# A hybrid attention and RWKV-7 layer: output weights split in two parts during the dense projections, kept in DRAM and loaded in parts in attention's first two tiles

## Chip, cores and metric

The kernel runs on one core of a Trainium2 chip. The metric is the device time of one execution in microseconds; a kernel's figure is the median of its timed runs. The engines named below are PE (TensorE, matmuls, with its weight loads PEld), DVE (VectorE), ACT (ScalarE), POOL (GpSimd) and SP (SyncE), which here only issues DMAs.

## What is computed

One layer on 1024 tokens of width 1024: RMSNorm, one input projection, eight heads of sparse attention beside eight heads of RWKV-7 time mixing, each times a SiLU gate, one output projection, a residual add and a last RMSNorm. Cut to what matters here:

```python
h = rms_norm(x, norm_g)
q, kc, vc, ks, vs, kw, vw, gl, g_nsa, rwkv_in, g_rwkv = split(h @ w_in)
o_nsa = nsa_mixer(q, kc, vc, ks, vs, kw, vw, gl, ...) * silu(g_nsa)
o_rwkv = rwkv7_mixer(rwkv_in, ...) * silu(g_rwkv)
mix = concatenate([o_nsa, o_rwkv])          # 1024 wide
return rms_norm(x + mix @ w_out, final_g)   # w_out: 1024 x 1024
```

All dense products are done in two parts: a float32 matrix is rounded to a high part (type fp32r), and the low part is the float32 matrix less the high one. A product takes three matmuls: high times high, low times high, high times low.

## The kernel before

**Projections.** After the norm, 29 groups of 128 output columns run on PE (`wda k0 k1 r0 r1 v0 v1 r2 k2 r3 k3 ...`), each 48 matmuls: two halves of 512 tokens, eight blocks of 128 input rows, three matmuls each. `Filler.weights` (L365) looks at the count of matmuls issued in the running group and serves the next one. At 2 it issues `fetch` of the first half of the next weights (a DMA of 256 KB into `wr`, which has one buffer), at 22 `split` and the fetch of the second half, at 40 the second `split`. `split` (L339) is an ACT copy (`k1h<-k1r`) and a DVE subtraction (`k1l<-k1r,k1h`), both made to wait for that matmul. The raw buffer is single, so a fetch waits for the subtraction ahead of it: four links, fetch, split, fetch, split, turn round once in each group. The second half of a group's weights is first used by its 13th matmul. Around these groups lie the RWKV pieces of the first head pairs (`wkv_elementwise`, `wkv_products`), and later, in the eight chains of the RWKV state, the groups fill PE between the links.

**Attention.** Eight tiles of 128 queries in the order 1, 5, 4, 3, 6, 2, 7, 0 (L1396), each with two branches (b = 0 and 1). A step of a branch is scores (`pst`), exponentials on ACT (`prob`), values (`po`) and sums of exponentials on POOL (`acc`). Beside these steps lie side pieces, put in at given shares of the branch: row maxima of the next branch (`ps`, `pd` on PE, `bm` and `nm` on DVE, turned by PE as `pnm`), the compressed branch (`pcs`, `pct`), the end of the branch before (`pz`, `rr`, `wide` on POOL, turned by PE as `prt`), the RWKV half of the mix (`mix_rwkv`: loads `yr` and `sg`, a POOL product, two ACT copies, a DVE subtraction `ml`) and, from the third tile, the output product (`output`, L1138).

**Output weights.** `load_w_out` (L1102) brings the eight blocks of `w_out` as raw 512 KB tiles (`wor`, two buffers shared with the residual `xt`), makes the high part on ACT (`woh`) and the low part on POOL (`wol`), four blocks in each branch of the second tile (`side.add(wout, 4)`, L1493). The output products of the first tile, in the third, are the first to read them.

**Order.** PE's order in attention is that of the program. The order of the other engines comes from a scheduler, which works from a model of the times; on the chip it is fixed. Every DMA is issued by SP, in order, so a DMA whose data are not ready holds up all behind it.

## Time and profile before

| what | value |
|---|---|
| timed runs | 1052.12, 1043.89, 1053.36 us; median 1052.12 us |
| profiled execution, its own time | 1040.26 us |
| its span | 1038.5 us, mean granted clock 0.951 |
| busy in the span | PE 930.2 us (90%), DVE 584.0, POOL 448.2, ACT 335.5 |
| moved by DMA | 115.66 MB, mean 111 GB/s |
| projections before the chains | about 50 to 185 us |
| attention | about 640 to 1015 us |

The engines run side by side and wait for each other by semaphores. PE is the fullest. A page of the profile shows how busy each engine was in 40 slices of the span, the DMA rate and the clock granted to TensorE (1.00 is its upper level of 2.4 GHz, 0.50 its lower of 1.2). The timelines show every instruction with its start, and in brackets how long its engine had been idle before it and what ended that. The chain of waits is followed back from the last instruction to whatever released each step.

### The profile page before, as it was taken

To read this page: it belongs to the slowest core of one execution; us is meant where nothing else is said; L and a number is where in the kernel's file an instruction comes from. 1 tells how busy PE (TensorE), PEld (TensorE's weight loads), DVE (VectorE), ACT (ScalarE), POOL (GpSimd) and SP (SyncE) were. 2 spreads that over 40 slices of the span, in tenths; PEclk is the share of its full clock that TensorE was granted. 3 is DMA by queue.
4 is the path that set the end of the run, shared out by engine and by line. 5 is a ranking of instruction groups with operands and counts; after the bars stand their busy time and mean duration, and the time that the engine had idled before them with its cause. 6 is when DMAs were issued, how large, how long until landed. Compare 5 with 4: busy or idle time off the path is not lost.

```text
span 1038.5 us, 17087 instructions
## 1 busy us (share of the span) xinstructions
PE 930.2 (90%) x6353; PEld 658.6 (63%) x6353; DVE 584.0 (56%) x1245; ACT 335.5 (32%) x650; POOL 448.2 (43%) x732
## 2 busy tenths in 40 slices
PE   5999999989998999899669978689999999889976
PEld 4888777766676766677458756354565656455555
DVE  7533545555575657374424335677659856685544
ACT  5533233224233443243121212433333333224321
POOL 3100153466483847444521120577463555246521
PEclk9999999999999999799889988879999999899989
DMA  7433453424426453536476293741132312231121
GB/s 259 125 102 102 125 157 108 130 76 116 135 76 172 134 154 119 131 106 170 116 218 192 65 203 95 212 122 31 41 63 79 77 46 69 53 80 33 39 84 41
DMA packets 154429, 115.66 MB, mean 111 GB/s; under 512 B 54369, under 2 KB 132266, under 8 KB 154346
## 3 DMA queue, kind: packets, MB, share of 16 engines
q1 hardware_dynamic: 154346, 114.57, 40.3%
q8 instruction: 50, 0.82, 0.3%
q14 instruction: 33, 0.27, 0.1%
HBM read 76.19 MB, written 35.19 MB: 107 GB/s over the span
## 4 chain that ended last, share of the span: by engine, by line
PE 60%; DVE 10%; DMA 9%; POOL 7%; SPq 6%; issue 5%; ACT 2%; POOLq 0%; DVEq 0%; ACTq 0%
PE pout L113 7%; SPq L85 6%; PE pst L113 6%; PE po L113 5%; PE p_r L113 4%; PE p_k L113 3%; PE p_gn L113 3%; PE p_gr L113 3%; PE p_q L113 3%; PE pc L113 2%; POOL lt L586 2%; POOL ltmp L584 2%; PE ps L113 2%; PE pd L113 2%; PE pcm L113 2%
## 5 line engine op out<-in xcount | busy, mean ns | idle before, releaser
L584 POOL TENSOR_TENSOR ltmp<-la,lt 128x60 f32<-128x60 f32 (+24 forms) x248 | 83.7, 337 | 65.3 <-DMA la<-dA 42.7
L1042 ACT ACTIVATE prob<-pst 128x512 f32<-128x512 f32 x132 | 74.6, 593 | 109.9 <-PE pst L113 106.3
L1055 POOL TENSOR_TENSOR acc<-acc,prob 128x1024 f32<-128x1024 f32 x36 | 86.7, 2409 | 45.1 <-ACT prob L1042 44.9
L586 POOL TENSOR_TENSOR lt<-lt,ltmp 128x60 f32<-128x60 f32 (+24 forms) x248 | 87.6, 353 | 18.8
L113 PE MATMUL pst<-q,k 128*128 128x512 f32 (+1 forms) x264 | 82.3, 430 | 0.0
L994 DVE TENSOR_REDUCE bm<-ps 128x6 f32<-128x384 f32 (+1 forms) x106 | 63.5, 613 | 26.6 <-PE ps L113 26.0
L113 PE MATMUL po<-prob,vt 128*64 128x512 f32 x264 | 75.1, 648 | 0.0
L1055 POOL TENSOR_TENSOR acc<-prob 128x1024 f32<-128x1024 f32 x14 | 33.7, 2410 | 82.6 <-ACT prob L1042 82.6
L113 PEld LDWEIGHTS pst<-q,k 128*128 128x128 f32 (+1 forms) x264 | 48.9, 196 | 14.9 <-issue 5.7
L113 PE MATMUL pout<-woh,mh 128*128 128x512 f32 x128 | 57.6, 450 | 0.2 <-DVE xt L1153 0.2
L113 PE MATMUL ps<-k,q 128*128 128x384 f32 (+3 forms) x136 | 45.4, 386 | 7.7 <-DVE bm L994 3.7
L113 PE MATMUL pout<-wol,mh 128*128 128x512 f32 x128 | 51.3, 401 | 0.0
L113 PE MATMUL pout<-woh,ml 128*128 128x512 f32 x128 | 51.2, 400 | 0.0
L113 PEld LDWEIGHTS ps<-k,q 128*128 128x128 f32 x136 | 25.6, 205 | 35.2 <-DVE bm L994 14.3
L982 DVE TENSOR_REDUCE bm<-pd 128x8 f32<-128x512 f32 x40 | 27.4, 688 | 26.2 <-PE pd L113 26.0
L113 PEld LDWEIGHTS pout<-woh,mh 128*128 128x128 f32 x128 | 25.1, 196 | 20.7 <-issue 17.8
L683 ACT ACTIVATE x<-pc 64x128 f32<-64x128 f32 x32 | 8.7, 272 | 75.4 <-DVE x L682 75.2
L113 PE MATMUL pd<-k,q 128*128 128x128 f32 x160 | 31.1, 321 | 2.1 <-POOL k L868 2.1
L1077 POOL TENSOR_TENSOR wide<-rr,ones 128x512 f32<-128x512 f32 x16 | 17.1, 1068 | 36.1 <-DVE rr L1073 34.1
L1069 DVE TENSOR_REDUCE zz<-pz 128x4 f32<-128x512 f32 x32 | 21.8, 684 | 13.4 <-PE pz L1067 13.0
L1153 DVE TENSOR_TENSOR xt<-pout,xt 128x512 f32<-128x512 f32 x16 | 11.1, 691 | 32.4 <-PE pout L113 32.4
L113 PEld LDWEIGHTS pd<-k,q 128*128 128x128 f32 x160 | 25.9, 204 | 4.0 <-POOL k L868 2.4
(518 smaller groups left out, 2447.7 us busy)
## 6 DMA issues: line engine op xcount, KB each, us to landing
dM<-mix SPq DMA_DIRECT2D x24, 256.0 KB
q<-dQH SPq DMA_DIRECT2D x22, 256.0 KB
la<-dA SPq DMA_DIRECT2D x32, 128.0 KB
xt<-in_x_dram SPq DMA_DIRECT2D x8, 512.0 KB
out_dram<-xt SPq DMA_DIRECT2D x16, 256.0 KB
x<-in_x_dram SPq DMA_DIRECT2D x7, 512.0 KB
mixk<-dM SPq DMA_DIRECT2D x8, 256.0 KB
mixr<-dM SPq DMA_DIRECT2D x8, 256.0 KB
```

What stands on the lines that cost most here:

```text
L85: return nc.sync.dma_start(plain(o), plain(i))
L113: return T.matmul(o, l, r, start=start, stop=stop)
L584: G.tensor_tensor(tv, la[:, j:j + 1, j + 1:].to_broadcast([128, m, n]), lt[:, :m, j:j + 1].to_broadcast([128, m, n]), op=OP.mult)
L586: G.tensor_tensor(lt[:, :m, j + 1:], lt[:, :m, j + 1:], tv, op=OP.add)
L683: gate["A"] = A.activation(x1[1][HP[1], c:8:4, :], pv[HP[1], :, 64:128], AF.Copy)
L982: V.tensor_reduce(bm[:, g * 4:g * 4 + 4, j:j + 2], p.rearrange("p (r b c) -> p r b c", b=2, c=64), axis=AX.X, op=OP.max)
L994: V.tensor_reduce(bm[:, h0:h0 + n, j:j + 2 * w], p[:, :n * w * 128].rearrange("p (h b c) -> p h b c", h=n, c=64), axis=AX.X, op=OP.max)
L1042: A.activation(pr[:, g * 512:(g + 1) * 512], p, AF.Exp)
L1055: G.tensor_tensor(s, self.acc, pr, op=OP.add)
L1069: V.tensor_reduce(zz[:, g, :], p.rearrange("p (r k) -> p r k", r=4), axis=AX.X, op=OP.add)
L1077: G.tensor_tensor(wide, rr.rearrange("p r g -> p (r g)").unsqueeze(2).to_broadcast([128, 8, 64]), ones64.unsqueeze(1).to_broadcast([128, 8 ...
L1153: V.tensor_tensor(xt[:, hs], p, xt[:, hs], op=OP.add)
```

## The change

A new generator, `split_w_out`, reads `w_out` in 16 parts of 128 x 512, makes the high part on ACT and the low part on DVE, and stores both to DRAM (`dWH`, `dWL`). Its tiles take one turn of the three buffers of `g0`, `g1` and `ar`, which the RWKV pieces use later; the two column halves of a tile alternate, and the load of the next part is issued ahead of the split of this one. `Filler.weights` calls it at the counts 12 and 34 of every group after the first. In attention `load_w_out` now only loads the two parts of each block (512 KB each), two blocks in each branch of the first two tiles, each load made to wait for the last exponential issued (`last_exp`). The raw tile `wor`, the ACT copies and the POOL subtractions there are gone.

```diff
--- before.py
+++ after.py
@@ -225,6 +225,7 @@
     dY = dram.tile([4, 128, S], FT, name="dY")
     dM = [dram.tile([4, 128, S], FT, name=f"dM{i}") for i in range(3)]
     dSR = dram.tile([4, 128, S], FT, name="dSR")
+    dWH, dWL = (dram.tile([8, 128, D], FR, name=n) for n in ("dWH", "dWL"))
 
 
     hh = [pj.tile([128, 8, 512], FR, name=f"hh{i}") for i in range(2)]
@@ -361,8 +362,11 @@
 
         def __init__(self, groups):
             self.groups, self.at, self.gen, self.i, self.cut = groups, -1, None, 0, None
+            self.extra = iter(())
 
         def weights(self, ins):
+            if self.at > 0 and self.i in (12, 34):
+                next(self.extra, None)
             if self.at + 1 == len(self.groups):
                 return
             g = self.groups[self.at + 1]
@@ -789,6 +793,36 @@
                     dma(v[:, hf * 8:hf * 8 + 8, :], t[hf * 64:hf * 64 + n])
             yield
 
+
+    def split_w_out():
+
+
+        wn = w_out.rearrange("l (n x) c -> (l n) x c", x=512)
+        raw, wh, wl = (r2(t, 3, (128, 8, 2, 64)).rearrange("p a b c -> p (a b c)")
+                       for t in ("g0", "g1", "ar"))
+
+        def load(k, cs):
+            o = raw[:, cs]
+            if k < 4:
+                for g in range(2):
+                    r0 = g * 256 + k * 64
+                    dma(o[g * 64:g * 64 + 64], wn[0, r0:r0 + 64, cs])
+            else:
+                dma(o, wn[1, (k - 4) * 128:(k - 3) * 128, cs])
+
+        parts = [(k, slice(h, h + 512)) for k in (4, 5, 6, 7, 0, 1, 2, 3) for h in (0, 512)]
+        load(*parts[0])
+        yield
+        for n, (k, cs) in enumerate(parts):
+            if n < 15:
+                load(*parts[n + 1])
+            h_ = wh.bitcast(FR)[:, cs]
+            A.activation(h_, raw[:, cs], AF.Copy)
+            l_ = wl.bitcast(FR)[:, cs]
+            V.tensor_tensor(l_, raw[:, cs], wh[:, cs], op=OP.subtract)
+            dma(dWH[k][:, cs], h_)
+            dma(dWL[k][:, cs], l_)
+            yield
 
     def compress(b, w1, w2):
         kc = []
@@ -1039,7 +1073,7 @@
                 mm(p, K2[b, g][:, w], L["q2", b][:, gh, :], start=False, stop=mask is None)
                 if mask is not None:
                     mm(p, identb, maskb[:, mask:mask + 1, :].to_broadcast([128, 4, 128]), start=False)
-                A.activation(pr[:, g * 512:(g + 1) * 512], p, AF.Exp)
+                last_exp[0] = A.activation(pr[:, g * 512:(g + 1) * 512], p, AF.Exp)
 
         def values(self, kt):
             if kt == 0:
@@ -1099,20 +1133,13 @@
 
     wo_h, wo_l = {}, {}
 
+    last_exp = [None]
+
     def load_w_out():
-        wn = w_out.rearrange("l (n x) c -> (l n) x c", x=512)
         for k in (4, 5, 6, 7, 0, 1, 2, 3):
-            raw = f4([128, D], FT, "wor")
-            if k < 4:
-                for g in range(2):
-                    r0 = g * 256 + k * 64
-                    dma(raw[g * 64:g * 64 + 64, :], wn[0, r0:r0 + 64, :])
-            else:
-                dma(raw, wn[1, (k - 4) * 128:(k - 3) * 128, :])
-            h_, l_ = w4([128, D], FR, "woh"), w4([128, D], FR, "wol")
-            A.activation(h_, raw, AF.Copy)
-            G.tensor_tensor(l_, raw, h_.bitcast(FT), op=OP.subtract)
-            wo_h[k], wo_l[k] = h_, l_
+            wo_h[k], wo_l[k] = w4([128, D], FR, "woh"), w4([128, D], FR, "wol")
+            for t, d in ((wo_h[k], dWH), (wo_l[k], dWL)):
+                behind(dma(t, d[k]), last_exp[0])
             yield
 
     xr = x.rearrange("b (n p) d -> (b n) p d", p=128)
@@ -1278,6 +1305,7 @@
         cp = pool(cmp_stack, "cp", "right")
 
     cp = None
+    filler.extra = split_w_out()
     filler.through("r1")
     for n in range(2):
         wkv_load(n, (0, 1))
@@ -1490,8 +1518,8 @@
                         side.add(compressed(j, L1), 3, 0.0, 0.9)
                 elif n < 7:
                     side.add(row_max(j, 0, L1), row_max_pieces(j, 0), 0.0, 0.8)
-                if n == 1:
-                    side.add(wout, 4)
+                if n < 2:
+                    side.add(wout, 2)
                 if n > 1:
                     side.add(outs[n - 2], 8)
                 if b == 1:
```

PE's order is the same but for a stretch between about 80 and 260 us, where RWKV pieces (`pss`, `pw`, `pp`, the first `pc`) stand some 10 to 15 matmuls later among the groups' matmuls. Three places matter.

First, SP in the projections, from the first fetch of group k1's weights to the first of r0's. `aS`, `wS` and `dM` are results that are stored away; `g<-in_w_out`, `dWH` and `dWL` are the new loads and stores. Before:

```order
L85 DMA k1r<-in_w_in_dram 128x4x128
L85 DMA aS<-st 64x512
L85 DMA wS<-st 64x512
L85 DMA k1r<-in_w_in_dram 128x4x128
L85 DMA dM_106<-mix 128x512
L85 DMA r0r<-in_w_in_dram 128x4x128
```

With the change:

```order
L85 DMA k1r<-in_w_in_dram 128x4x128
L85 DMA dWH<-g_820 128x512
L85 DMA dWL<-ar 128x512
L85 DMA g_819<-in_w_out_dram 128x512
L85 DMA aS<-st 64x512
L85 DMA wS<-st 64x512
L85 DMA dWH<-g_820 128x512
L85 DMA dWL<-ar 128x512
L85 DMA g_819<-in_w_out_dram 128x512
L85 DMA k1r<-in_w_in_dram 128x4x128
L85 DMA dWH<-g_820 128x512
L85 DMA dM_106<-mix 128x512
```

Six new DMAs stand between the two fetches of k1, and as many again between the second of them and r0's first. In all, 24 loads and 32 stores go between k0's first fetch and v1's first.

Second, SP where attention begins, from the load of the last norm's weights. Before:

```order
L85 DMA fg<-in_final_g_dram 128x1024
L85 DMA yr<-dY 128x4x128
L85 DMA sg<-dSR 128x4x128
L85 DMA wor<-in_w_out_dram 128x1024 x2
L85 DMA sg<-dSG 128x4x128
L85 DMA sg<-dSR 128x4x128
```

With the change:

```order
L85 DMA fg<-in_final_g_dram 128x1024
L85 DMA woh<-dWH 128x1024
L85 DMA wol<-dWL 128x1024
L85 DMA woh<-dWH 128x1024
L85 DMA wol<-dWL 128x1024
L85 DMA yr<-dY 128x4x128
L85 DMA sg<-dSR 128x4x128
L85 DMA woh<-dWH 128x1024
L85 DMA wol<-dWL 128x1024
L85 DMA sg<-dSG 128x4x128
L85 DMA xt<-in_x_dram 128x1024 x2
```

The four loads of the first two blocks now stand ahead of `yr` and the first `sg`, and the two raw loads behind these are gone.

Third, DVE in the same place, at the row maxima of tile 5 and the end of the first branch. Before:

```order
L1069 TENSOR_REDUCE zz<-pz 128x4
L1126 TENSOR_TENSOR ml<-yr,mh 128x512
L994 TENSOR_REDUCE bm<-ps 128x4x2 x2
L1004 TENSOR_TENSOR bm<-bm,nm_6505 128x4x12 x2
L1006 TENSOR_REDUCE nm_6505<-bm 128x8
L1009 TENSOR_TENSOR q_6549<-pnm,keep 40x1024
L1069 TENSOR_REDUCE zz<-pz 128x4
L1072 RECIPROCAL zz<-zz 128x8
L1073 TENSOR_TENSOR rr<-zz,gt 128x2x4
```

With the change:

```order
L1103 TENSOR_REDUCE zz<-pz 128x4
L1028 TENSOR_REDUCE bm<-ps 128x4x2 x2
L1038 TENSOR_TENSOR bm<-bm,nm_6598 128x4x12 x2
L1040 TENSOR_REDUCE nm_6598<-bm 128x8
L1043 TENSOR_TENSOR q_6642<-pnm,keep 40x1024
L1103 TENSOR_REDUCE zz<-pz 128x4
L1153 TENSOR_TENSOR ml<-yr,mh 128x512
L1106 RECIPROCAL zz<-zz 128x8
L1107 TENSOR_TENSOR rr<-zz,gt 128x2x4
```

The subtraction `ml` stood ahead of the maxima that `pnm` waits for; now it stands behind them, ahead of `rr`.

## Rows read from the trace of the kernel before

**Rows 1.** The page: the span in 40 slices, busy share in tenths, below GB/s.
```profile
PE   5999999989998999899669978689999999889976
...
PEclk9999999999999999799889988879999999899989
```

**Rows 2.** Stretches: length, busy time by engine, granted clock, DMA share, GB/s.
```profile
50.00:80.00 30.00, 30.00 (x138) 25.00 (x137) 9.73 (x15) 10.53 (x18) 1.12 (x7) 1.00 0.34 93
80.00:110.00 30.00, 30.00 (x136) 24.09 (x135) 11.28 (x27) 9.64 (x18) 2.17 (x8) 1.00 0.35 106
650.00:700.00 50.00, 35.32 (x146) 22.00 (x144) 35.90 (x57) 19.66 (x30) 33.37 (x17) 0.77 0.60 167
```

**Rows 3.** Chain of waits, 653 to 675 us: start, length, what.
```profile
653.47 6.44 DMA sg<-dSR
...
663.02 1.47 POOL wol L1114
...
674.88 1.12 PE prt L1081 x4
```

**Rows 4.** Timeline of PE: start, length, what, idle before and its end.
```profile
670.82 0.46 PE L1008 MATMUL pnm<-ident,nm 128*104 128x128 f32 x1 [7.83 <-DVE nm L1006]
...
674.88 1.12 PE L1081 MATMUL prt<-ident,wide 128*128 128x128 f32 x4 [0.85 <-POOL wide L1077]
...
695.74 1.12 PE L950 MATMUL pct<-ident,pc 128*128 128x128 f32 x4 [4.89 <-DVE pc L945]
```

**Rows 5.** Timeline of DVE in attention's first tiles.
```profile
663.98 1.94 DVE L1126 TENSOR_TENSOR ml<-yr,mh 128x512 fp32r<-128x512 f32 x1 [1.10 <-ACT mh L1125]
...
667.04 3.44 DVE L1004 TENSOR_TENSOR bm<-bm,nm 128x48 f32<-128x48 f32 x2
...
673.53 0.17 DVE L1073 TENSOR_TENSOR rr<-zz,gt 128x8 f32<-128x8 f32 x1
...
689.19 1.98 DVE L1073 TENSOR_TENSOR rr<-zz,gt 128x8 f32<-128x8 f32 x1
...
695.77 2.20 DVE L929 TENSOR_TENSOR imh<-sp 128x32 f32<-128x32 f32 x1
...
701.91 1.94 DVE L1095 SCALAR_TENSOR_TENSOR t<-t,sg 128x512 f32<-128x512 f32 x1
```

**Rows 6.** Instructions on tile wor: ns min/median/max, first and last start.
```profile
L85 SPq DMA_DIRECT2D wor<-in_w_out_dram x12: 346/484/598, 654.0 to 691.7; - x12
L1113 ACT ACTIVATE woh<-wor x8: 1042/1054/1057, 661.9 to 700.3; 128x1024 fp32r<-128x1024 f32 x8
L1114 POOL TENSOR_TENSOR wol<-wor,woh x8: 2335/2368/2814, 663.0 to 703.3; 128x1024 fp32r<-128x1024 f32 x8
```

**Rows 7.** The view of rows 2, four other stretches.
```profile
110.00:114.00 4.00, 4.00 (x19) 3.31 (x18) 3.93 (x6) 0.59 (x2) 1.32 (x2) 1.00 0.79 256
134.00:138.00 4.00, 4.00 (x32) 3.04 (x31) 0.75 (x1) 1.66 (x3) 0.00 (x0) 1.00 0.78 185
658.00:662.00 4.00, 3.34 (x17) 2.04 (x16) 2.98 (x5) 0.90 (x3) 1.29 (x1) 1.00 0.90 332
671.00:683.00 12.00, 11.15 (x36) 6.44 (x36) 5.69 (x8) 5.07 (x8) 8.70 (x6) 0.50 0.62 168
```

**Rows 8.** Timeline of all engines: two weight fetches and their splits.
```profile
68.79 0.37 SPq L85 DMA_DIRECT2D k1r<-in_w_in_dram  x1
...
71.94 0.63 ACT L342 ACTIVATE k1h<-k1r 128x512 fp32r<-128x512 f32 x1 [3.33 <-DMA k1r<-in_w_in_dram]
...
72.61 0.69 DVE L344 TENSOR_TENSOR k1l<-k1r,k1h 128x512 fp32r<-128x512 f32 x1 [3.13 <-ACT k1h L342]
...
72.87 0.39 PE L113 MATMUL p_k<-hh,k1h 128*128 128x512 f32 x1
...
73.33 0.37 SPq L85 DMA_DIRECT2D r0r<-in_w_in_dram  x1
...
78.28 0.63 ACT L342 ACTIVATE r0h<-r0r 128x512 fp32r<-128x512 f32 x1 [4.47 <-PE p_k L113]
```

## The prediction

> **What bounds the kernel now.** I read first the page's slices: PE is busy in nine tenths or more of most slices. It falls to 6 tenths in slices 20, 21 and 26, and the change works in the last of these, 650 to 675 us, where the granted clock stands at 8 tenths and goes to 7 in the next [rows 1]. Then the stretches, because the change works in two of them. From 50 to 110 us PE is busy all the time at the full clock while the DMA engines are busy for a third of it [rows 2]: this stretch is bound by PE, and anything that stops PE there is paid in full. From 650 to 700 us PE is busy for 35.3 of 50 us at a clock of 0.77, POOL for 33.4 and the DMA engines for 60% [rows 2]: here PE waits. Who it waits for is in the chain of waits: the load of `sg`, then POOL and its `wol` subtractions, until PE turns `wide` at 674.9 us [rows 3]. PE's own timeline gives the sizes: 7.83 us for `nm`, 0.85 us for `wide`, 4.89 us for `pc` [rows 4].
>
> **What is removed from attention.** Eight ACT copies of 1.05 us (8.4 us) and eight POOL subtractions of 2.37 us, 20 us with the long ones [rows 6]. Off the path these are worth nothing; what counts is what waits for them. Three places do.
>
> (a) The wait for `nm`. PE's last `ps` ended 7.83 us before 670.82, at 663.0 [rows 4]. Behind it DVE did `ml` in 1.94 us, for which it had waited 1.10 us, and two additions over 48 columns in 3.44 us while POOL was in `wol` [rows 3, 5]. With the change `ml` stands behind `nm`, and POOL has one sum of exponentials to do there and no subtraction. DVE then needs two reductions no larger than the 0.69 us of 512 columns [rows 8], two small additions at about the 0.17 us of `rr` [rows 5] and `nm`: some 2 us, so `pnm` runs near 665 instead of 670.8.
>
> (b) That does not carry all the way, because the next wait, for `wide`, hangs on `ml`, and `ml` on `yr` and `sg`. These two loads now stand behind four loads of 512 KB. `sg` landed at 653.47 + 6.44 = 659.9 us [rows 3]; 2.1 MB more at the 332 GB/s of that moment [rows 7] are 6.3 us, so 666.2. From there to PE: POOL's product (half of 2.37 us [rows 6]), two ACT copies of 0.63 and a DVE subtraction of 0.69 [rows 8], 0.4 us of small DVE steps, `wide` at again half of 2.37, and handing over: about 5 us, so 671.3 instead of 674.9, a gain of **3.6 us**. Bounds: if the loads cost `sg` nothing, the part behind `nm` alone leaves PE at about 668.6, a gain of 6.3; if they go at the 185 GB/s of a stretch with small pieces [rows 7], `sg` lands near 671.3 and the gain is -1.5.
>
> (c) The clock. After the empty 8 us the clock stood at 0.50 from 671 to 683 us, and PE was busy for 11.15 of these 12 us [rows 7]; at the full clock the same work is 5.6 us. With the hole cut in two, of about 2 and 4 us, it may or may not fall. The bounds are 0 and 5.6; nothing shows which, and I take the middle, **2.8 us**.
>
> (d) The DVE chain that ends in `pct` and the next `nm`, 684 to 706 us. Single operations there took 1.98, 2.20 and 1.94 us [rows 5] where the same or the same size takes 0.17, 0.17 and 0.69 [rows 5, 8], an excess of 5.1 us. Two more of the same kind (`ml`, and `pc`, which I put at 1.3 and 0.7 us by the same comparison) bring it to some 7 to 8. The last four of the eight `wol` fall into these 22 us (they end with the one at 703.3 [rows 6]), and about as many sums `acc` of the same size, which stay. So half, **4 us**; the bounds are 2 and 8. The row shows DVE held while POOL runs. The Trainium skill (SBUF — State Buffer, Who interferes with whom) states that a DVE instruction with two SBUF inputs and a GpSimd instruction that reads SBUF exclude each other for the whole instruction. By that rule what is saved goes with POOL's busy time, and taking seven `wol`, 17 of its 33.4 us in 650 to 700, out of it gives an estimate of 3.9 us; the trace agrees in kind, and the sum above does not use it.
>
> Together attention gives 3.6 + 2.8 + 4 = **10.4 us**, bounds 0.5 to 20. The extra loads behind this (8.4 MB instead of 4.2, over four branches) lie beside other work: after 700 us the DMA engines have room, since the old kernel's raw loads ended at 691.7 [rows 6].
>
> **What is added to the projections.** Sixteen ACT copies at 0.63 us and sixteen DVE subtractions at 0.69 us [rows 8], 10 and 11 us in a stretch of 60 us in which ACT is busy for 20 and DVE for 21 [rows 2]: no engine becomes full, so they cost nothing of themselves. They are covered by PE's matmuls, and each only delays a split by 0.6 to 0.7 us.
>
> The DMAs are another matter, through SP's order and the DMA engines. The weight loop has this slack: the second fetch of k1 is issued at 68.79, its ACT copy starts at 71.94, the subtraction ends at 73.30, the next fetch goes at 73.33 [rows 8]. k1 starts on PE at 72.87 [rows 8], and its 13th matmul, the first to need that half, comes 12 times 0.22 us later (136 to 138 matmuls in 30 us [rows 2]) at 75.5: slack 2.2 us. The other half lands by the same 3.15 us at 76.5 and is then held until PE has come to its place at 78.28 [rows 8]: slack 1.8. Together 4.0 us, once.
>
> The new transfers are 4.2 MB of loads and 8.4 MB of stores, within nine fetch intervals (k0's second fetch to v1's first), each 24 matmuls or 5.3 us, together 47 us. They come on top of about 100 GB/s [rows 2], 4.7 MB: 17.3 MB. What rate the DMA engines reach on such a mixture is not shown; by share, 256 GB/s at 0.79 is 324, 185 at 0.78 is 237, 332 at 0.90 is 369 [rows 7]. I take 310, near the first of these, whose transfers are of the same kind (weights, `dM` stores, loads of 256 KB). Then 17.3 MB take 55.8 us, 8.8 more than there are; less the slack of 4.0, PE stops for **5 us** in all, a fraction of a microsecond to two at each group. Bounds: at 369 GB/s they fit in 46.9 us, cost 0; at 237 they take 73 us, cost 22.
>
> The Trainium skill (DMA: Bandwidth & Descriptors, Queues, rings and completion order) states that on each DMA engine descriptors are consumed in ring order. By that rule a fetch waits for every store issued ahead of it; it is the mechanism of the third rival, and this trace, with its DMA engines a third busy, does not yet show it.
>
> PE's own order moves too: RWKV pieces some 10 to 15 matmuls later. That is a swap, cost nothing as long as the groups' matmuls fill the place (PE is full there [rows 2]); without that cover it would be 13 times 0.22, 3 us.
>
> **Sum.** 5 - 10.4 is -5.4 us. Against the profiled execution's 1040.26 us that is 1034.9; the timed runs stand higher, their median at 1052.12, so I forecast **1046.7 us** there, which is inside the 1% that a measurement of this kernel can tell from no change (its timed runs differ by 0.9%).
>
> **Rivals.**
> 1. *The projections hide it all and the clock holds.* For it: PE's holes in attention are plain [rows 4], and DMA has room on average [rows 2]. Then 0 - (3.6 + 5.6 + 5) = -14 us, 1038 us.
> 2. *`sg` and `yr` come late.* The wait for `wol` gives way to one for the four loads ahead of them. For it: SP's order; against: 4 KB rows go fast. With (b) at -1.5 and (c) at 0, 5 - 2.5 = +2.5 us, 1054.6 us, no change. The same time comes out if the early weights change nothing that PE waits for, which is this change not doing what it says.
> 3. *The weight loop breaks.* In-order SP puts two `dWL`, each waiting for a load, a copy and a subtraction, ahead of every fetch, and the engines behind it saturate. At 237 GB/s PE loses 22 us; attention gives back 10: +11.6 us, 1063.7 us. It is the side where the kernel gets slower, and it decides once the rate on this mixture is below about 240 GB/s.
>
> **Chances and range.** The forecast 0.35, rival 1 0.33, rival 2 0.15, rival 3 0.17. Faster by over 1%: rival 1 and a little of the forecast, 0.36; slower by over 1%: rival 3, 0.17; within 1%: 0.47. The range runs from 1052 less 20 (attention at its best, projections free), 1032, with two for the scatter of the runs below it, to 1059, which is a loss of 12 in the projections with a gain of 5 in attention; the forecast's own range is 1040 to 1052.
>
> **What would show it.** In the changed profile, 50 to 110 us: PE busy less than the length, with p_k, p_r or p_v waiting for a split, confirms the 5 us; a DMA share of 0.9 or more there the mechanism; a PE still full refutes it. At 660 to 675: `pnm` near 665 and `prt` near 671; a `prt` waiting on `ml` after a late `yr` is rival 2. At 671 to 683: the granted clock. At 684 to 706: `rr`, `imh` and `t` back at 0.2 to 0.7 us. The forecast is wrong if attention begins later by over 10 us, or not later at all, or if the hole of slice 26 only moves.

## The result, and the profile after

The changed kernel is slower: 1050.61 us against 1045.61 us (medians of 20 runs each, side by side), and the ratio of the runs is 1.0075, with an interval of 1.0053 to 1.0096: about 8 us, more than the 5.0 us between the medians. That is inside the 1% that was called no change, and on the other side of the 5.4 us of gain that was forecast. That 1050.61 us lies in the range given, and within 4 us of the forecast, is luck: the forecast started from the median of three runs, 1052.12 us, and twenty give 1045.61. Ratios leave out executions that are slower at a lower clock, and the profiled one of those runs was such a one, so the profile shown here is of the same kernel run once more (label a_again). Its span is 1049.4 us against 1038.5.

The two rows of the page that answer [rows 1], 40 slices of 26.2 us:

```profile
PE   5899999988999999899679968769999999889976
...
PEclk9999999997989999899889988969999999899989
```

The 6 of slice 26 (counted from 1) is now a 7 and a 6 in slices 26 and 27: the hole has moved along with attention's later start, it hasn't gone. The stretches that answer [rows 2], one more among them (columns as there):

```profile
50.00:80.00 30.00, 28.93 (x132) 23.18 (x131) 13.12 (x20) 13.23 (x23) 0.94 (x6) 1.00 0.83 270
80.00:110.00 30.00, 29.04 (x128) 22.91 (x127) 14.82 (x31) 12.29 (x22) 0.95 (x6) 1.00 0.98 316
180.00:250.00 70.00, 60.81 (x538) 43.33 (x537) 34.68 (x71) 19.23 (x42) 29.83 (x79) 0.91 0.41 113
650.00:700.00 50.00, 40.38 (x177) 25.70 (x175) 23.59 (x50) 13.30 (x24) 11.26 (x8) 0.90 0.73 207
```

From 50 to 110 us PE lost 2.0 of 60 us, and the DMA engines went from a third to 0.83 and 0.98 busy. The loss of the projections stands mostly elsewhere: from 180 to 250 us PE is busy for 60.8 us, and in the kernel before for 65.46. From 650 to 700 us PE looks better, and POOL's 33 us of work are down to 11; but part of this is only that attention begins 11 us later in the window. From the end of the projections to the end of attention's second tile (660.7 to 718.3 us, before 649.9 to 706.8) PE is busy for 39.36 of 57.6 us, and was for 40.58 of 56.9; POOL is busy for 20.31 us, and was for 39.66.

A table of positions says where the time goes. The first row is the profile of before, in us; the others are how much later the same event is than there. *pss* is the first instruction of RWKV's first unit, *v3* and *gr3* the ends of those groups (gr3 is the last of the projections), *pnm* the transposition of `nm` that stands at 706.8 us before, where attention's first two tiles end, and *end* the span. *Att.* is pnm less gr3: what attention's first two tiles gained (-) or lost.

| kernel | pss | v3 | gr3 | pnm | end | att. | ratio to before, interval |
|---|---|---|---|---|---|---|---|
| before (us) | 89.2 | 251.0 | 649.9 | 706.8 | 1038.5 | | |
| before_again | +1.5 | +3.1 | +4.3 | +3.9 | +5.6 | -0.4 | one run |
| a_again (the change) | +8.1 | +13.9 | +10.8 | +11.5 | +10.9 | +0.7 | 1.0074, 1.0035 to 1.0114 |
| proj_only | +8.2 | +14.5 | +17.8 | +18.0 | +19.4 | +0.2 | 1.0085, 1.0052 to 1.0118 |
| proj_dma | +9.9 | +20.0 | +18.4 | +24.6 | +23.7 | +6.1 | 1.0115, 1.0046 to 1.0184 |
| proj_small | +8.5 | +13.2 | +10.4 | +9.9 | +10.1 | -0.5 | 1.0058, 1.0023 to 1.0092 |
| proj_quarter | +4.7 | +10.6 | +10.5 | +16.4 | +15.4 | +5.9 | 1.0096, 1.0062 to 1.0129 |
| late_rwkv | +11.3 | +4.0 | +3.4 | +7.9 | +6.7 | +4.5 | 1.0068, 1.0030 to 1.0107 |
| pinned_before | +2.8 | +6.0 | +11.4 | +17.0 | +15.7 | +5.5 | 1.0100, 1.0068 to 1.0133 |
| pinned_late | +7.0 | +10.2 | +15.6 | +5.9 | +8.0 | -9.8 | 1.0030, 0.9994 to 1.0067 |
| pool_queue | +2.4 | +9.2 | +18.8 | +9.2 | +7.7 | -9.6 | 1.0058, 1.0028 to 1.0087 |
| slow_late | +3.6 | +9.4 | +15.9 | +7.9 | +6.1 | -8.0 | 0.9990, 0.9953 to 1.0027 |
| half_late | +4.4 | +4.6 | +4.3 | -2.0 | +1.1 | -6.3 | 1.0018, 0.9984 to 1.0053 |
| gn16 | +2.9 | +4.4 | +23.9 | +14.0 | +12.9 | -9.9 | 1.0075, 1.0039 to 1.0110 |
| split8 | +3.6 | +5.4 | +22.3 | +15.2 | +13.4 | -7.1 | 1.0046, 1.0017 to 1.0074 |
| att_only | +1.4 | +1.4 | -1.6 | -1.4 | -1.5 | +0.2 | 0.9965, 0.9927 to 1.0003 |
| att_late | +1.3 | +3.1 | +4.3 | -3.4 | -6.0 | -7.7 | 0.9876, 0.9824 to 0.9927 |
| after_late | +9.2 | +14.8 | +14.4 | +3.4 | +2.3 | -11.0 | 0.9986, 0.9962 to 1.0009 |

Two rows say how far one profile can be trusted. before_again is the kernel before, and it is 3 to 6 us later from v3 on. att_only and att_late differ in the place of attention's loads alone, and stand 5.9 us apart at gr3. So a shift of gr3 under some 6 us is nothing by itself; what repeats over several kernels (pss, v3, att.) is. Every shift also holds an earlier one: the group k0 starts 1.1 to 3.7 us later than before in all the other profiles, also in those without early work (1.5 in before_again, 2.9 in gn16); in a_again it is 1.1.

**So the change is two halves**: projections that lose 11 to 18 us in the profiles (9 us in the runs), and an attention that gains nothing.

### The profile page after: what moved, and what is told of

It reads as the page before. It is cut to its first block, busy times and chain, and to the rows that moved or that the text cites. A ratio compares the mean times of both kernels' runs of the same rounds, so it can differ in the third digit from the quotient of the medians.

```text
span 1059.4 us, 17231 instructions
## 1 busy us (share of the span) xinstructions
PE 943.6 (89%) x6353; PEld 667.1 (63%) x6353; DVE 590.2 (56%) x1261; ACT 336.9 (32%) x658; POOL 426.6 (40%) x724
## 4 chain that ended last, share of the span: by engine, by line
PE 45%; DMA 17%; DVE 11%; POOL 9%; issue 6%; SPq 5%; ACT 2%; POOLq 0%; DVEq 0%; ACTq 0%
PE pout L113 7%; PE pst L113 6%; PE po L113 5%; SPq L85 5%; POOL lt L590 3%; POOL ltmp L588 3%; PE p_gr L113 3%; PE ps L113 2%; PE pc L113 2%; PE p_kc L113 2%; PE pd L113 2%; PE p_gn L113 2%; PE pcm L113 1%; DMA dM<-mix 1%; PE p_ks L113 1%
## 5 line engine op out<-in xcount | busy, mean ns | idle before, releaser
L113 PE MATMUL ps<-k,q 128*128 128x384 f32 (+3 forms) x136 | 45.4, 386 | 10.4 <-DVE bm L1016 6.5
L113 PEld LDWEIGHTS ps<-k,q 128*128 128x128 f32 x136 | 25.5, 204 | 37.7 <-DVE bm L1028 13.9
L1016 DVE TENSOR_REDUCE bm<-pd 128x8 f32<-128x512 f32 x40 | 27.4, 688 | 23.3 <-PE pd L113 23.1
```

What stands on the lines that cost most here:

```text
L113: return T.matmul(o, l, r, start=start, stop=stop)
L1016: V.tensor_reduce(bm[:, g * 4:g * 4 + 4, j:j + 2], p.rearrange("p (r b c) -> p r b c", b=2, c=64), axis=AX.X, op=OP.max)
```

## The experiments

### The two halves apart

**a_again** has no edit.

> The changed kernel itself, once more, for a profile to read beside that of the kernel before. Theory P (the projections lose and attention gives back a part): the group v3 ends 13 to 20 us later than before, attention's stretch is 5 to 10 us shorter, the whole 1.005 to 1.010 of before. Theory A (attention gains nothing, the projections lose little): v3 ends about 8 us later and attention is as long as before.

It came out at 1.0074: v3 13.9 us later, as Theory P said. But attention isn't shorter (+0.7), as Theory A said. Each was half right.

**proj_only** keeps the projections' part and takes attention back to raw loads, ACT copies and POOL subtractions:

```
-            for t, d in ((wo_h[k], dWH), (wo_l[k], dWL)):
-                behind(dma(t, d[k]), last_exp[0])
+            A.activation(h_, raw, AF.Copy)
+            G.tensor_tensor(l_, raw, h_.bitcast(FT), op=OP.subtract)
```

> The kernel before with the split and its stores added to the projections; attention loads and splits the weights as it did, so that what is stored is not read. Theory P: 1.012 to 1.018 of before (12 to 19 us), as attention gives nothing back. Theory A: 1.006 to 1.009, as the changed kernel. If the loss were PE waiting for the groups' own weights (the prediction's term), PE would stand idle in front of k1 to v1 by 50 to 115 us; if it is the RWKV unit that starts late, PE stays full there and the first pss comes 8 to 10 us later.

1.0085 is the size that Theory A gave, but v3 and gr3 are 14.5 and 17.8 us late, as Theory P had it; the second profile of before (end of this part) shows how much of the 17.8 may be scatter. The first pss is 8.2 us late with PE busy for 57.5 of the 60 us from 50 to 110, so RWKV's unit does start late, and PE standing idle makes up less than half of it.

**att_only** has all of attention's loads from one stored block, and a single part split in the projections:

```
-                behind(dma(t, d[k]), last_exp[0])
+                behind(dma(t, d[4]), last_exp[0])
```

> The changed kernel's attention without the projections' part: one part of the sixteen is split and stored, and all sixteen loads of attention read that one block, with the same number and size of transfers (so the output weights are not the right ones). Theory P, with the prediction's terms: 10 us faster, 0.990 of before (bounds 0.5 to 20 us). Theory A: 0.998 to 1.002. In the trace: pnm near 665 and prt near 671 us if the prediction's steps for attention hold; rr, imh and t at 0.2 to 0.7 us.

0.9965, with an interval that takes in 1. Up to prt the forecast's steps hold to half a microsecond: pnm runs at 663.0 us and prt at 669.95, counted from gr3's end 6.2 and 3.3 us earlier than before (5.8 and 3.6 forecast). By the next pnm nothing is left of it. The chain of waits of att_only (start, length, what) tells why:

```profile
668.60 0.18 DVE rr L1106
...
671.50 12.63 DMA yr<-dY
...
687.42 1.50 DVE ml L1152
...
689.39 1.76 DVE rr L1106
```

The second tile's `yr` is issued at 671.5 and is there 12.63 us later. In the kernel before it was issued at 665.94, and POOL used it at 671.43. Now it stands in SP's order and on the DMA engines behind eight 512 KB loads, those of the first tile's two branches.

### Attention's loads later

**att_late** is att_only with the eight pairs placed where the kernel before had its loads:

```
-                if n < 2:
-                    side.add(wout, 2)
+                if n == 1:
+                    side.add(wout, 4)
```

> As the kernel with attention's part alone, but all eight pairs of loads are placed in the second tile (four in each branch, where the kernel before had its loads) instead of over the first two tiles. Theory Y (the second tile's yr stands behind the 512 KB loads for 12.6 us and takes back what the first tile gains): yr lands within 7 us of its issue, pct at 696 and the next pnm come 4 to 6 us earlier than before, 0.993 of before. Theory O (what comes behind is DVE's chain, whatever yr does): no more than with the loads early, 0.996 to 1.000.

0.9876, from four runs. Theory Y holds, and by more than it said. PE's four waits in this part show the difference. First PE's timeline of the changed kernel (a_again), then of att_late; behind each instruction the idle time before it and what ended it:

```profile
675.44 0.32 PE L1042 MATMUL pnm<-ident,nm 128*104 128x128 f32 x1 [1.66 <-DVE nm L1040]
...
682.42 1.11 PE L1115 MATMUL prt<-ident,wide 128*128 128x128 f32 x4 [5.22 <-POOL wide L1111]
...
706.59 1.12 PE L984 MATMUL pct<-ident,pc 128*128 128x128 f32 x4 [8.22 <-DVE pc L979]
...
718.28 0.32 PE L1042 MATMUL pnm<-ident,nm 128*104 128x128 f32 x1 [1.03 <-DVE nm L1040]
```

```profile
670.73 0.32 PE L1041 MATMUL pnm<-ident,nm 128*104 128x128 f32 x1 [3.49 <-DVE nm L1039]
...
676.00 1.12 PE L1114 MATMUL prt<-ident,wide 128*128 128x128 f32 x4 [2.25 <-POOL wide L1110]
...
694.27 0.66 PE L983 MATMUL pct<-ident,pc 128*128 128x128 f32 x4 [2.40 <-DVE pc L978]
...
703.43 0.32 PE L1041 MATMUL pnm<-ident,nm 128*104 128x128 f32 x1 [0.39 <-DVE nm L1039]
```

Before, the first three were 7.83, 0.85 and 4.89 us [rows 4] and the fourth this:

```profile
706.82 0.32 PE L1008 MATMUL pnm<-ident,nm 128*104 128x128 f32 x1 [1.67 <-DVE nm L1006]
```

The four sum to 15.2 us before, 16.1 in the changed kernel and 8.5 in att_late. The change moved the hole from pnm to prt and pct; placing the loads later closes half of it. Its cause is `yr` and `sg`, in the chains of waits of a_again (two rows) and att_late (two rows):

```profile
667.24 10.13 DMA sg<-dSR
...
684.52 12.42 DMA yr<-dY
```

```profile
657.77 6.43 DMA sg<-dSR
...
668.05 5.50 DMA yr<-dY
```

The Trainium skill (DMA: Bandwidth & Descriptors, Queues, rings and completion order) states that on each DMA engine descriptors are consumed in ring order. These rows agree: the same 256 KB take 12.4 us behind the 512 KB loads and 5.5 us ahead of them.

**after_late** is the whole change with that one edit.

> The changed kernel with one edit: attention's eight pairs of loads in the second tile (four in each branch) instead of over the first two. If the two parts simply add, projections as in the changed kernel (gr3 ends 11 us later than before) and attention 10 us shorter: 0.997 to 1.002 of before. If the measured 0.988 of attention's part alone is the truth and the 1.0085 of the projections' alone too, 0.996.

0.9986, as forecast for two parts that simply add: with attention's 11 us the loss of the projections is made good, and nothing is over. By the two ratios that is 0.9% better than the change as it was made; from the kernel before it can't be told apart.

### Bytes, or the place in the queue

**proj_dma** leaves out the copies and subtractions, **proj_small** of these transfers three quarters of the bytes (32 of 128 rows):

```
-            A.activation(h_, raw[:, cs], AF.Copy)
-            V.tensor_tensor(l_, raw[:, cs], wh[:, cs], op=OP.subtract)
-            dma(dWH[k][:, cs], h_)
-            dma(dWL[k][:, cs], l_)
+            dma(dWH[k][:, cs], raw[:, cs])
+            dma(dWL[k][:, cs], raw[:, cs])
```

> As the kernel with the projections' part alone, but without the sixteen copies and sixteen subtractions: each raw part is stored twice as it was loaded (nothing reads it). Theory D (the transfers and their places in SP's order make the loss): the same loss as with them, within 0.3%. Theory E (ACT and DVE wait in their order for a raw part, and the groups' splits and mix behind them): at most a third of that loss, 1.004 or less.

> As the kernel with the projections' transfers alone, the same number of them at the same places, but each of a quarter of the bytes (32 of 128 rows). Theory B (the bytes fill the DMA engines and every transfer takes longer): at most a third of that kernel's loss, 1.004 of before or less, and dM to mixk as fast as before. Theory N (the number of transfers in SP's order makes it): the same loss, 1.009 to 1.012.

1.0115, from four runs, as Theory D said; and 1.0058, between Theory B's 1.004 and Theory N's 1.009. The transfers alone are enough for the loss. But both carry a wait that the change doesn't have: `raw` is itself what is stored, so the load after next waits for those stores on SP. **proj_quarter** has all copies and subtractions and no such wait, with a quarter of the bytes in every load and store:

```
-                dma(o, wn[1, (k - 4) * 128:(k - 3) * 128, cs])
+                dma(o[0:32], wn[1, (k - 4) * 128:(k - 4) * 128 + 32, cs])
...
-            dma(dWH[k][:, cs], h_)
+            dma(dWH[k][0:32, cs], h_[0:32])
```

> The projections' part alone with all its copies, subtractions, loads and stores at the same places, but every load and store moves 32 of 128 rows, a quarter of the bytes (what is stored isn't read). It differs from the earlier kernel with small transfers in that a load need not wait for stores. Theory B (bytes): at most a third of the 1.0085 of the projections' part, 1.003. Theory N (number and place in SP's order): 1.006 to 1.010.

1.0096, not less than with all the bytes (1.0085): Theory N's number, and not Theory B's 1.003. But the two profiles lose in different places. Up to gr3 proj_quarter loses 10.5 us and proj_only 17.8; in attention's two tiles proj_quarter loses 5.9 and proj_only 0.2, and these 5.9 come in kernels without small transfers too (end of this part). So the equal ratios don't show that the bytes cost nothing. Its stretches (columns as in [rows 2]) show that the DMA engines have room:

```profile
50.00:80.00 30.00, 29.52 (x135) 23.70 (x135) 14.12 (x22) 14.37 (x27) 1.06 (x6) 1.00 0.51 135
80.00:110.00 30.00, 29.54 (x128) 22.75 (x127) 15.17 (x33) 13.42 (x25) 2.50 (x8) 1.00 0.53 155
```

The bytes do count for something: pss is 4.7 us late and not 8.2, v3 10.6 and not 14.5. Some two thirds of the shift at v3 are there without them. Nor is it the bytes alone that differ, because the scheduler puts pss elsewhere in PE's order: after 120 matmuls of the groups before, 135 in the change and proj_only, 125 in proj_dma, 120 in proj_small and 124 in proj_quarter. The clearest case against the bytes comes below, in pool_queue.

What the transfers do in SP's order is plain in SP's own timeline, first of before, then of a_again. The event is the third `dM` store, after which `mixk` of RWKV's first units can be loaded:

```profile
80.38 0.34 SPq L85 DMA_DIRECT2D dM<-mix  x1
83.57 0.88 SPq L85 DMA_DIRECT2D mixk<-dM  x2
```

```profile
86.44 0.54 SPq L85 DMA_DIRECT2D dM<-mix  x1
87.03 0.47 SPq L85 DMA_DIRECT2D g<-in_w_out_dram  x1
...
88.72 1.36 SPq L85 DMA_DIRECT2D g<-in_w_out_dram  x2
90.54 0.89 SPq L85 DMA_DIRECT2D mixk<-dM  x2
```

`dM` goes 6.1 us later and `mixk` 7.0. Some 3.4 of the 6 us come from PE, whose `p_k` for this `mix` ends that much later (1.1 of it is k0's start). The rest comes from ACT and DVE: DVE's `mix` stands behind the subtraction of a part, which waits for that part's load and ACT's copy. DVE's timeline of a_again:

```profile
84.15 0.69 DVE L822 TENSOR_TENSOR ar<-g,g 128x512 fp32r<-128x512 f32 x1 [2.57 <-ACT g L820]
84.76 0.69 DVE L345 TENSOR_TENSOR r0l<-r0r,r0h 128x512 fp32r<-128x512 f32 x1
85.36 0.74 DVE L418 SCALAR_TENSOR_TENSOR mix<-p_k,dv,mt 128x512 f32<-128x512 f32 x1
```

Yet PE doesn't wait for `mixk` at pss. In PE's timeline, of before (first row) and of a_again (second), pss has no idle time before it:

```profile
89.20 0.95 PE L113 MATMUL pss<-mi,s 128*128 128x2 f32 x8
```

```profile
97.33 0.95 PE L113 MATMUL pss<-mi,s 128*128 128x2 f32 x8
```

It runs when its place in PE's order comes, 15 matmuls of 0.226 us later than before. So the 8.1 us are 1.1 of k0's later start, 3.4 of place, and 3.6 that PE lost in the groups ahead of it. At the old place PE would have waited about 1.2 us for `mixk` and the ACT operation behind it, by an estimate from these rows and the end of that operation at 95.2 us.

### Why 8 us become 14

**late_rwkv** holds back `mixk` in the kernel before, and nothing else:

```
-            wkv_load(n, (0, 1))
+            wkv_load(n, (0, 1), filler.mark["r0", 34])
```

> The kernel before with one dependency more and nothing else: the loads of mixk for the first two RWKV units wait for a matmul of the group r0, so that the first pss comes some 8 us later, as it does in the changed kernel. Theory R (what costs in the projections is the late start of the RWKV units, whose chain of DVE, POOL and small transfers ends last): v3 ends 11 to 15 us later, the whole is 1.008 to 1.012 of before. Theory W (it is PE waiting for the groups' weights and the transfers in its way): at most 4 us, 1.004.

Theory R falls: pss is 11.3 us late, and v3 only 4.0. A late start alone is mostly made up by 250 us. (The runs' 1.0068 fits neither theory. The profiled execution, 1047.02 us, is faster than their median of 1051.30, and of its 6.7 us 4.5 come in attention, to which I return.) What differs is PE's order. In the kernel before the two `pp` of the second unit stand after 423 and 443 matmuls of the groups, in the changed kernel after 438 and 458, in both behind the first `px`, which needs the end of the first unit's solve on POOL. In late_rwkv the scheduler put them after 413 and 435, ahead of `px`. PE's timeline of a_again at that place, with PE waiting at `px` and then in front of the six matmuls that were put ahead of `pp`:

```profile
181.00 0.24 PE L113 MATMUL px<-t,cr 32*32 32x32 f32 x2 [0.94 <-DVE t L637]
182.23 0.50 PE L113 MATMUL p_k<-hh,k3h 128*128 128x512 f32 x1 [0.99 <-DVE mix L418]
...
185.13 0.80 PE L113 MATMUL pp<-ar,bk 64*128 64x128 f32 x4
...
193.10 1.17 PE L113 MATMUL pp<-ar,bk 64*128 64x128 f32 x16
```

The first of them ran at 175.44 before, the second at 182.96: 9.7 and 10.1 us earlier, where the first unit was then only 4.2 us late (its `pvt`, 145.8 and 149.9). What hangs on it is the second unit's solve on POOL, 31 us of small instructions, which begins like this in before (first row) and in a_again (second):

```profile
195.90 0.24 POOL L584 TENSOR_TENSOR ltmp<-la,lt 128x31 f32<-128x31 f32 x1 [5.72 <-DMA la<-dA]
```

```profile
206.06 0.24 POOL L588 TENSOR_TENSOR ltmp<-la,lt 128x31 f32<-128x31 f32 x1 [4.12 <-DMA la<-dA]
```

At its end PE waits for what the solve gives, in front of the second unit's `px`, which ran at 232.7 us before:

```profile
243.28 0.24 PE L113 MATMUL px<-t,cr 32*32 32x32 f32 x2 [2.12 <-DVE t L637]
```

The shift is not steady: 4.2 us at the first `pvt`, 10 at the second unit's `pp`, 6.3 at the `pn` of 215.3 us, 10.6 at this `px`, 13.9 at v3.

**pinned_before** and **pinned_late** write the order of before out by hand, for the kernel before and for after_late:

```
+    with tc.manual_schedule(engines={mybir.EngineType.PE}):
+        upto(96)
+        for n in range(2):
+            wkv_load(n, (1,))
+        el, pro = wkv_elementwise(0), wkv_products(0)
+        upto(120)
+        hp(el, 2)
...
+        upto(423)
+        hp(prod)
```

> The changed kernel with attention's loads in the second tile, and PE's order from k0 to k3 written out by hand as it stands in the kernel before (the first pss after 120 matmuls of the groups, pp of the second unit after 423 and 443, ahead of px), instead of where the scheduler puts these pieces when it has counted the added transfers (135, 438 and 458). Theory S (the order frozen on PE, with the second unit's pp behind px, makes the shift grow from 8 to 14 us between 140 and 250 us): the shift of 7 to 9 us at the first pss stays as it is, v3 ends at most 9 us late, the whole is 0.990 to 0.995 of before. Theory T (the units are late because their transfers are, whatever PE's order): v3 13 us late or more, 0.997 to 1.001.

> The kernel before with the same order of PE written out by hand, and nothing else: what the writing out costs by itself. Both theories: v3 within 2 us of before, 0.998 to 1.002.

Writing it out costs 1% by itself, against both theories, so only the difference speaks. Nor is it quite the order of before: the second unit's first `pp` stands ahead of the first `px` in both, and behind it in the kernel before. With the order fixed, the added work makes pss 4.2 us later (7.0 less 2.8), v3 4.2 (10.2 less 6.0) and gr3 4.2 (15.6 less 11.4): a shift that stays what it is. Without it 8.1 us at pss are 13.9 at v3. half_late (below) says the same without a pinned order: the scheduler left PE's order alone there, and 4.4 us at pss are 4.6 at v3. That the order makes the growth is shown so far, in one profile of each kernel. The runs can't tell it: beside att_late's 0.9876, with its loads at the same place, the added work costs 1.1% in the scheduler's order (0.9986) and 0.6% in the fixed one (1.0030 over 1.0100), and the intervals of these ratios are 0.2 to 0.5% to either side. How much hangs on this one place isn't shown.

### Other places for the same work

**pool_queue**: after_late, with the parts' transfers issued by POOL.

```
+    def dma2(o, i):
+        return nc.gpsimd.dma_start(plain(o), plain(i))
```

> As the kernel just named, but the sixteen parts' loads and stores are issued by POOL, which has little to do from 50 to 110 us, instead of SP. Theory N (what costs is the place of these transfers in SP's order, ahead of the groups' weights, dM and mixk): the first pss at most 4 us late, gr3 at most 4 us, 0.990 to 0.994 of before. Theory B (the bytes fill the DMA engines, whoever issues them): dM to mixk as slow as in the changed kernel, the first pss 8 us late, 0.996 to 1.000.

Off SP's queue pss is only 2.4 us late, with all the bytes: 1.3 of k0's start and 0.9 of a place four matmuls later. PE is busy for all of the 60 us from 50 to 110, at a DMA share of 0.78 and then 0.91. That part of Theory N holds, and Theory B falls for what PE lost there; gr3, 18.8 us late, and the ratio are not what Theory N said. Each issue takes POOL some 0.54 us. POOL also copies a column of `mt` for every group, and its order has changed too: that copy now stands behind a wait for `mixr`, and `mix` and PE wait for it. POOL's timeline, and PE's waits from 105 to 145 us (what, for whom, total, times, longest):

```profile
116.22 1.29 POOL L521 TENSOR_TENSOR ar<-mixr,s 128x512 f32<-128x512 f32 x1 [5.37 <-DMA mixr<-dM]
117.45 0.25 POOL L416 COPY mt<-last 128x1 f32<-128x1 f32 x1
```

```profile
PE p_v L116 <- DVE mix L421: 4.2, 1, 4.2
```

v3 is 9.2 us late again, and the whole is 1.0058. Moving the transfers to another engine's order moved waits with them.

**slow_late**: half the pace, from k0 to kw, in the `st` buffers.

```
-            if self.at > 0 and self.i in (12, 34):
+            if self.at > 0 and self.i in (4, 30):
```

> The whole change, with the sixteen parts at half the pace (one part in each group from k0 to kw, in the four buffers that mix uses) and attention's loads in the second tile only. Theory B (bytes in too short a time): the first pss no more than 4 us late, v3 no more than 6, attention 4 to 6 us shorter than before: 0.998 to 1.002 of before. Theory N (their number in SP's order, now also between the small transfers of the RWKV chains): v3 at least 10 us late, 1.006 or more.

pss is 3.6 us late (2.9 of it k0's start), but v3 9.4 and gr3 15.9, so Theory B's bound for v3 fails, and Theory N's 10 is just missed. The parts now stand among the small transfers of the chains; that these are what they delay isn't shown. With attention's 8 us it is 0.999, no change, as Theory B's number had it.

**half_late**: eight parts in the projections; blocks 0 to 3 are loaded raw and split in attention.

```
-        parts = [(k, slice(h, h + 512)) for k in (4, 5, 6, 7, 0, 1, 2, 3) for h in (0, 512)]
+        parts = [(k, slice(h, h + 512)) for k in (4, 5, 6, 7) for h in (0, 512)]
```

> As the kernel with loads in the second tile, but only the four blocks k 4 to 7 are split in the projections (eight parts, over by 85 us); blocks 0 to 3 are loaded raw and split in attention's second tile by ACT and POOL as before. PE's order in the projections is then that of the kernel before. Theory B and N alike: gr3 at most 4 us later than before; attention: 5 us shorter if each pair counts alike, 10 if only the first four subtractions of POOL were in the way: 0.993 to 0.998.

gr3 is 4.3 us late (at most 4 forecast) and attention 6.3 shorter (5 to 10 forecast); the runs say 1.0018, no change, and not the 0.993 to 0.998 forecast.

**gn16** puts all parts into the last eight groups, **split8** eight early and eight there.

```
-            if self.at > 0 and self.i in (12, 34):
+            if self.groups[self.at].name[:2] in ("gn", "gr") and self.i in (2, 14, 26, 38):
```

> The whole change with the sixteen parts moved from k1 to v1 (60 to 110 us) to the last eight groups gn1 to gr3 (455 to 650 us), two parts in each, in the buffers that the silu results use; attention's loads in the second tile. PE's order before 450 us is that of the kernel before. Theory S (the loss came from RWKV's first units and the order that the scheduler froze for them): no shift up to 450 us, gr3 at most 4 us late, attention 10 us shorter: 0.988 to 0.994 of before. Theory T (sixteen loads and thirty-two stores cost 8 us or more wherever they stand): 0.996 or more.

> As the kernel just named, but eight parts early (k 4 to 7, 55 to 85 us, as in the kernel with half the parts, where gr3 came 4 us late) and eight in gn1, gn0, gr0 and gr1. Theory S: gr3 4 to 6 us late, attention 10 us shorter, 0.992 to 0.996 of before. Theory T: 0.997 or more.

Theory S doesn't carry this far. Up to gn1 gn16 is 5.7 us late, within what two profiles of one kernel differ by; by gr3 it is 23.9. PE's waits from 450 to 670 us, of gn16, then of before:

```profile
PE pd L113 <- DVE bm L1024: 9.4, 1, 9.4
...
PE p_gn L113 <- ACT gn2h L343: 6.9, 1, 6.9
...
PE p_gn L113 <- DVE gn2l L345: 4.1, 1, 4.1
...
PE p_gn L113 <- ACT gn3h L343: 2.8, 1, 2.8
```

```profile
PE p_gn L113 <- DVE gn2l L344: 4.9, 1, 4.9
...
PE p_gn L113 <- ACT gn2h L342: 4.1, 1, 4.1
PE ps L113 <- DVE bm L982: 3.1, 2, 3.0
```

A part of the loss is the groups' own weights that come late, the wait that the prediction looked for between 50 and 110 us: 13.8 us in gn2 and gn3, and 9.0 before. A larger part is the 9.4 us for `bm`, a row maximum, where the kernel before waits 3.0. That reduction stands in DVE's order right behind the subtraction of a part, and the subtraction had waited for the part's load and copy (DVE's timeline of gn16):

```profile
649.16 0.69 DVE L818 TENSOR_TENSOR wol<-wor,woh 128x512 fp32r<-128x512 f32 x1 [16.85 <-ACT woh L817]
```

It is what `mix` met in the early place, at a dearer spot. So the work costs something wherever it was put: Theory T holds as to the amount (gn16 1.0075, split8 1.0046 with gr3 22.3 us late), Theory S as to how it comes about in the early place. No version here that splits all the weights beats the kernel before.

**before_again** has no edit.

> The kernel before once more, for a second profile: how far two profiles of one kernel lie apart in each stretch. The profile shown of before lies 5 us under the median of its runs; if what its slower runs lose is lost in attention's first two tiles, the new profile differs there and not before 650 us.

Its 5.6 us come in several places (1.5 by k0's start, 3.1 by v3, 6.0 by the end of the group kc1, 4.3 at gr3) and not in attention's first two tiles (-0.4), so the expectation was wrong. Yet the old attention does have a dearer form: in proj_dma, proj_quarter, late_rwkv and pinned_before its two tiles take 4.5 to 6.1 us more than in before, and in the others with the old splits (proj_only, proj_small, before_again) -0.5 to 0.2. The late loads have shown no such form, which may be why att_late's runs gain 13 us where its profile gains 10.3 from gr3 to the end; what chooses the form was not tried.

## Why the prediction was wrong, step by step

**The 5 us of the weight loop: near in size, wrong in its reason.** PE lost 3.6 us in the groups ahead of the first pss, and the signs that were named for it came: 29.0 of 30 us busy, a DMA share of 0.98. But it was reckoned from bytes at 310 GB/s, and the signs don't tell bytes from place. proj_quarter, with a quarter of the bytes, still loses 2.6 us from k0's start to r1's end, where proj_only loses 3.6; pool_queue, with all of them in another queue, at a share of up to 0.91, loses nothing. The Trainium skill's ring order (same section as above) was the right kind of rule; whether the place that mattered was in the rings or in SP's order of issue, no run here separates, since pool_queue changed both.

**PE's own order, "a swap, cost nothing": the step that failed in the projections.** The prediction took the groups' matmuls as a cover, and 3 us for the case without one. For PE they nearly are one: it was busy for 58.0 of 60 us. What they don't cover is the chain of RWKV units behind those pieces, from DVE over `dM`, `mixk` and small transfers to POOL's solve. The runs showed in its place: the move costs pss 3.4 us, the second unit's `pp` comes 10 us later and POOL's solve 10.2, PE waits for it, and v3 ends 13.9 us late; with PE's order held, the same added work costs 4.2 us at pss, v3 and gr3 alike. I followed a weight fetch through SP's queue and not the `dM` stores and `mixk` loads in that same queue: `mixk` is issued 7.0 us later. That the scheduler moved the RWKV pieces because its model counted this is likely, and not shown. The same blind spot made ACT's and DVE's added work free ("they cost nothing of themselves"): DVE's subtraction is 0.69 us, but it waited 2.57 us in front of `mix`.

**(a) and (b), attention's first tile: right.** Taken from gr3's end, pnm came 6.2 us earlier in both a_again and att_only (5.8 forecast) and prt 3.3 us (3.6 forecast). `sg` took 10.13 us from its issue instead of 6.44 [rows 3] and landed at 677.4, 10.8 us of later start included: 666.2 was forecast.

**(c), 2.8 us of clock: nothing.** The clock fell all the same: the stretch of a_again that answers the last of [rows 7], behind a wait of 5.22 instead of 7.83 us for PE:

```profile
682.00:690.00 8.00, 7.58 (x24) 4.87 (x25) 2.08 (x3) 1.60 (x3) 1.64 (x2) 0.50 1.12 193
```

From gr3's end to the pnm at the end of the second tile the granted clock was 0.79 before and is 0.82 now; it is 0.82 in before_again too.

**(d), 4 us of DVE's chain: wrong in sign, by the step that failed in attention.** From prt to pct the kernel took 20.9 us before and takes 24.2 now. `rr` did come back, to 0.15 us, and other operations stayed slow with no `wol` left on POOL. DVE's timeline of a_again:

```profile
699.73 1.50 DVE L1153 TENSOR_TENSOR ml<-yr,mh 128x512 fp32r<-128x512 f32 x1 [2.93 <-ACT mh L1152]
701.15 2.82 DVE L953 TENSOR_TENSOR pc<-pc,z 128x512 f32<-128x512 f32 x1
704.38 0.15 DVE L1107 TENSOR_TENSOR rr<-zz,gt 128x8 f32<-128x8 f32 x1
...
711.42 2.85 DVE L1127 TENSOR_TENSOR t<-t,pos 128x512 f32<-128x512 f32 x1
```

The three of 512 columns and the next `t` (2.36 us) are 6.8 us over 0.69 each; the prediction counted 7 to 8 of such excess before. POOL's sums `acc` are there as before and now lie beside others of DVE's operations: in att_only `rr` took 1.76 us. The rule of the Trainium skill that the prediction used (SBUF — State Buffer, Who interferes with whom) fits that, but taking half of POOL's work out moved the clashes rather than halving them. The 3.3 us of (b) went back here, to `yr`. The prediction had the extra loads "lie beside other work", at no price; the second tile's `yr` took 12.42 us behind them instead of 5.5, and PE waited 8.22 us for `pct` instead of 4.89. **Rival 2** was the right mechanism, for the second tile where I looked at the first. Its bound of -1.5 for (b) was thus not the worst case: the loads delay a second `yr` as well. With `yr` in time (att_late) the way from prt to the next pnm takes 27.4 us, and it took 31.9 before and takes 35.9 in a_again: a gain of the size of (d) is there, and how much of it is clash and how much clock was not separated.

**The sum.** Forecast: 5 less 10.4; measured about +8 in the runs. Attention has the larger part of the 13 us between them: +0.7 instead of -10.4, and with the loads moved back (after_late) it is -11.0 and the whole 0.9986. The rest is the projections'. In the profile: 10.8 at gr3, past the 10 us that the prediction named as a sign of being wrong, and 0.7 in attention. Rival 3 named SP's order with its `dWL` stores, but put its price on PE stopping for 22 us in the weight loop at a rate under 240 GB/s. 316 GB/s flowed and PE lost 3.6 us there; the kernel is about 8 us slower all the same (11.6 in rival 3).

## What to carry to other kernels

Work that is moved under a stretch in which one engine is full is not free if that stretch also feeds another chain: look in the issuing queue for every transfer behind the added ones, not for the one whose engine is full. Ask of each load that is moved earlier which small load then stands behind it: eight large loads, the first of them used 76 us after its issue (663.7 and 739.8 us), cost the second tile's `yr` 7 us, and moving them back, with nothing else, won 11.7 us of attention's first two tiles in the profiles and 0.9% by the ratios. Choose a sign that rivals don't share: a full DMA and a PE that loses 2 of 60 us fitted the rate and the queue alike. And where a scheduler freezes an order from its own estimate, read that order again after the change.

## What the runs showed of the hardware that was not expected

Transfers of a quarter of the bytes in the same queue still held up the weight groups: from k0's start to r1's end they lost 2.6 us with stores of 64 KB, at a DMA share of 0.51 and 0.53, and 3.6 with stores of 256 KB, at 0.84 and 0.95 (proj_quarter and proj_only). The full 256 KB, issued by POOL at a share of 0.78 and 0.91, held them up by nothing, and each issue took POOL some 0.54 us. And two executions of one kernel stand 3 to 6 us apart from 250 us on (before and before_again), at the same clock to 0.004 (0.951 and 0.947).
